# Visits of four feature tiles instead of two for the conditioning products of a two-layer hybrid decoder step

## Chip, cores and metric

The kernel runs on one core of one Trainium2 chip. The metric is the device time of one execution in microseconds; less is better. The core's engines each work through a queue of their own, in order: TensorE (PE in the profile; its weight loads are PEld), VectorE (DVE), ScalarE (ACT), GpSimd (POOL) and SyncE (SP, which here only issues transfers). Times stand as the hardware profiler took them.

## What is computed

One step of a two-layer decoder trunk for 512 prompt tokens and 8 single-token samples, in float32. Each layer takes shift, scale and gate from a conditioning vector, normalises and modulates its input, projects it to the columns of four token mixers, runs these, and adds the gated output projection to the stream:

```python
mod = jax.nn.silu(c) @ ada_w[l] + ada_b[l]
shift, scale, gate = jnp.split(mod, 3, axis=-1)
h = rms_norm(x, norm_g[l]) * (1.0 + scale[:, None, :]) + shift[:, None, :]
proj = h @ w_in[l]
pa, pb, pc, pd = jnp.split(proj, [A_W, A_W + B_W, A_W + B_W + C_W], axis=-1)
...            # oA: HGRN2, oB: RWKV-7, oC: dilated attention, oD: multi-scale pooling
mix = jnp.concatenate([oA, oB, oC, oD], axis=-1).astype(x.dtype)
x = x + gate[:, None, :] * (mix @ w_out[l])
```

Here `c` is (9, 1024) for prompt and samples together, `ada_w[l]` is 1024 x 3072, `w_in[l]` 1024 x 3648 and `w_out[l]` 1024 x 1024. The change concerns the first line: `silu(c) @ ada_w[l]`.

## The kernel before

**Layout.** Features lie on the 128 partitions, tokens along the free side: 520 columns (512 prompt tokens, 8 samples), worked in two halves of 256 and 264. A feature tile is 128 of the 1024 model features, so every product over the model width is a sum over eight feature tiles.

**Projections.** `project` makes one 128-column block of `w_in` or `w_out` at a time. It is carried in three products per feature tile and half (high part of the input by high part of the weights, low by high, high by low), so a block is 48 matmuls ("pj" in the profile). Weights arrive in half blocks of 256 KB in `wraw` and are split into `whi` and `wlo` by ScalarE with GpSimd or with an accumulating transfer; each of these tags has four buffers (`FBUFS`). Loads of weights are issued by SP.

**Conditioning products.** `ada_part(l, f0, nf, spare, ahead, pin)` makes the shift and scale of `nf` feature tiles of layer l, or its gates for `nf == 8`. With 1024 columns it takes the eight feature tiles of `silu(c)` one by one: it loads 512 KB of `ada_w` (tile `adaw`, loaded from SP at L380) and multiplies in four column groups of 32 (`Q4`), which the profile shows as 8 instructions of the form 128*32 128x256 per feature tile, name "ada". The sum goes to SBUF (`adar`), is transposed (`adaT`) and becomes the factors (`mod`). With `ahead` of 1, as in the three parts below, each feature tile's load stands one step ahead of its products. These loads take buffers of the tag `big`, of which there are four; the transposed key caches (`ckT`) use the same tag later.

**The planner.** A layer's mixers are Python generators ("streams"). `Flow` interleaves them with the generator of the projections. A stream that yields `(cost, latency)` tells how much TensorE time, in ns, the step just emitted takes and how long until its next step has its inputs. The cost is added to a clock `t` and, times `RATIO` (1.11), to a debt; while the debt is positive, the planner emits projection steps, 660 each in the usual case, which lower it. Then it emits a step of the ready stream of the lowest priority number. A stream is ready again at `t + latency * LAT` (`LAT` is 1.3).

```python
        cost, lat = r[0:2]
        e[4] = len(r) == 2
        self.t += cost
        e[1] = self.t + lat * LAT
        self.debt = max(self.debt, -2000.0) + cost * self.ratio
```

In layer 0 the streams are B (priority 0), A, CS, C, D, and with the last priority, 5, first `ada_part(0, 0, 8)` (the gates of layer 0), then `ada_next(0)`, which runs `ada_part(1, 0, 4)` and after it `ada_part(1, 4, 4)` (shift and scale of layer 1). The first of these two and the gates can be open at once. Layer 1 has no such stream in its planner. The other conditioning parts are made outside the planner, with `ahead` of 2, 4 or 8, and are told apart by `ahead > 1`.

**The order on the engines.** What the planner emits is a program order. The framework (`schedule_with_timeline_sim=True`) then places each engine's instructions with a timeline of its own, so that an instruction whose inputs are late there is passed by later ones; the result is fixed per engine before the kernel runs. Buffers of a tag are handed out in that order, and a load into one waits, at SP, for its last reader.

Of the kernel before, what the change touches and what calls it, by code (L numbers as in the profile page):

```python
# [191 lines left out]
def trunk(ctx: ExitStack, tc: tile.TileContext, I, O):  # L192
# [28 lines left out]
    def half_t(name):  # L221
        return sb.tile([128, NT], F32, tag="h", name=name, bufs=FBUFS["h"])
# [7 lines left out]
    def sm_ps(name):  # L230
        return ps.tile([128, 512], F32, tag="sm", name=name, bufs=1)
# [10 lines left out]
    def add(out, a, b, eng=V):  # L242
        return tt(out, a, b, ALU.add, eng)
# [9 lines left out]
    def stt(out, a, s, b, op0, op1):  # L253
        return V.scalar_tensor_tensor(out=out, in0=a, scalar=s, in1=b, op0=op0, op1=op1)  # L254
# [5 lines left out]
    def copy(out, a):  # L260
        return A.activation(out, a, AF.Copy)  # L261
# [6 lines left out]
    def mm(out, lhsT, rhs, start=True, stop=True):  # L268
        return PE.matmul(out, lhsT, rhs, start=start, stop=stop)  # L269

    def bc(ap, shape):
        return ap.to_broadcast(shape)
# [40 lines left out]
    def P(l, name, j=0, n=1):  # L313
        a, _ = PCOL[name]
        return par[:, l, a + j:a + j + n]
# [44 lines left out]
    def ada_part(l, f0, nf, spare=0, ahead=1, pin=False):  # L360

        gates = nf == 8

        def pinned(ins):
            return tc.keep_in_program_order(ins) if pin else ins


        c0, width = (2048, 1024) if gates else (256 * f0, 256 * nf)  # L370

        nk = 2 if nf == 1 else 1
        W, kp = width * nk // 4, 1024 // width
        pt = (pj_ps if kp > 1 else sm_ps if l and gates else mm_ps)("ada")[:, 0:W]
        ws = []
        for i in range(8 // kp + ahead):
            if i < 8 // kp:
                w = (f1k if i < spare else big_t)("adaw")
                w = w.rearrange("p (k n) -> p k n", k=kp)
                load(w, I["ada_w"][l, :, i * kp:(i + 1) * kp, c0:c0 + width])  # L380
                ws.append(w)
            if i < ahead:
                if i == ahead - 1:
                    yield 0.0, 0.0
                continue
            for k in range((i - ahead) * kp, (i - ahead + 1) * kp):
                for g in range(4 // nk):
                    r4 = Q4[nk * g + k % nk]
                    mm(pt[r4, :], sc[:, k, :], ws[i - ahead][:, k % kp, W * g:W * g + W],
                       start=(k < nk), stop=(k >= 8 - nk))  # L390
            if ahead > 1:
                yield 450.0, 1500.0
            elif (i - ahead) % 2:
                yield 900.0, 3000.0
        raw = half_t("adar")[:, 0:W]
        pinned(copy(raw, pt))
        yield 0.0, 600.0
        nq = W // 128
        pT = sm_ps("adaT")[:, 0:128 * nq // nk]
        if nk == 1:  # L400
            for q in range(nq):
                PE.transpose(pT[:, q * 128:q * 128 + 128], raw[:, q * 128:(q + 1) * 128], ident)
        else:
            mm(pT, raw, pairs)
        n = 1 if gates else 2
        m = cst.tile([128, n, nf, 9], F32, name=f"mod{l}{f0}{nf}")

        src = pT.rearrange("p (q g f b) -> p f g q b" if nf == 4 else "p (q f g b) -> p f g q b", q=nq, b=32, f=n)
        for f in range(n):
            bias = P(l, "ada_b", 16 if gates else 8 * f + f0, nf).rearrange("p (g q) -> p g q", q=nq)  # L410
            add(m[:, f].rearrange("p (g q) b -> p g q b", q=nq), src[:, f, :, :, 0:9],
                bc(bias[:, :, :, None], [128, nf // nq, nq, 9]))
        if gates:
            modG[l] = m[:, 0]
        else:
            g = P(l, "norm_g", f0, nf)
            stt(m[:, 1], m[:, 1], 1.0, bc(g[:, :, None], [128, nf, 9]), ALU.add, ALU.mult)
            for k in range(nf):
                modS[l, f0 + k], modA[l, f0 + k] = m[:, 0, k, :], m[:, 1, k, :]
        yield 240.0, 600.0  # L420
# [1092 lines left out]
    def layer(l, xs, rstd, x_src, soon, scaled=None):  # L1513
# [49 lines left out]
        def split_projections():  # L1563
# [5 lines left out]
            def make(k):  # L1569
# [8 lines left out]
                if k in (1, 3, 5):  # L1578
                    scaled((k + 1) // 2)

            later = ada_part(l, 4, 4, 8, 8, True)

            def use_part(n, j):
# [17 lines left out]
            for half in range(2):  # L1601
                for gi, group in enumerate([tiles[0:FIRST[0]]] + [[e] for e in tiles[FIRST[0]:]]):
                    g = []
                    for name, _, M, _ in group:
                        n, j = (name, 0) if name == "wa" else (name[:2], int(name[2]))
                        g.append(((l, name), M, use_sum(name, n, j, M) if half else use_part(n, j)))
                    yield from project(g, xt, make if gi == 0 else None, 4 * half, 4 * half + 4)
                    if half:
                        for name, _, _, _ in group:
                            flow.done.add(name)  # L1610
                    else:
                        for _ in range(FIRST[0]):
                            next(later, None)
                if not half:
                    for _ in later:
                        pass
                    small_params()
                    for name in CONST_SHAPES:
                        if name not in C and name not in ("seg", "rope"):
                            load_const(name)  # L1620
                    flow.add(ada_part(l, 0, 8), 5)
# [61 lines left out]
        if not last:  # L1683
            soon = ada_part(l + 1, 0, 8, 4, 8)
            next(soon)
# [163 lines left out]
```

## Time and profile before

| | us |
|---|---|
| median of 3 runs | 762.91 |
| lowest and highest run | 761.4, 771.46 |
| the profiled execution, its own time | 762.74 |
| its span, first to last instruction | 760.9 |

The span is what the profile's rows cover; the execution's own time has 1.8 us more around it. Busy time is per engine, and engines overlap. A row of a timeline gives the start, the duration, the engine, the line and operation, and what is written from what; an "x8" says that eight instructions alike stand in a row, and a bracket how long the engine was idle before the row and what ended that. Matmuls overlap in the pipeline, so the distance between two starts tells what one costs, not its duration. PEclk is the granted share of TensorE's clock.

### The profile page before, as it was taken

To read this page: it belongs to the slowest core of one execution; us is meant where nothing else is said; L and a number is where in the kernel's file an instruction comes from. 1 tells how busy PE (TensorE), PEld (TensorE's weight loads), DVE (VectorE), ACT (ScalarE), POOL (GpSimd) and SP (SyncE) were. 2 spreads that over 40 slices of the span, in tenths; PEclk is the share of its full clock that TensorE was granted. 3 is DMA by queue.
4 is the path that set the end of the run, shared out by engine and by line. 5 is a ranking of instruction groups with operands and counts; after the bars stand their busy time and mean duration, and the time that the engine had idled before them with its cause. 6 is when DMAs were issued, how large, how long until landed. Compare 5 with 4: busy or idle time off the path is not lost. (4 is left out here: it accounts for less than half of the span.)

```text
span 760.9 us, 18617 instructions
## 1 busy us (share of the span) xinstructions
PE 691.9 (91%) x7297; PEld 615.1 (81%) x7297; DVE 505.1 (66%) x1183; ACT 457.6 (60%) x988; POOL 281.8 (37%) x326
## 2 busy tenths in 40 slices
PE   2899998997989899998998989898698999998997
PEld 1687777897889888877797889797697989787897
DVE  4547627989985454787456352995999763577863
ACT  5255787535645566895355899943264557688641
POOL 1344213427732223136326232454454232213641
PEclk9999999998999979999999999999798999999999
DMA  9968887887664539579794678799755448459575
GB/s 325 350 228 291 289 234 166 212 210 180 145 168 96 145 104 261 152 181 295 161 258 129 148 159 177 169 207 223 181 122 143 102 106 215 97 143 277 118 172 152
DMA packets 87608, 142.46 MB, mean 187 GB/s; under 512 B 20577, under 2 KB 29089, under 8 KB 87521
## 3 DMA queue, kind: packets, MB, share of 16 engines
q1 hardware_dynamic: 67216, 104.50, 42.6%
q0 software_dynamic: 20160, 36.71, 28.3%
q8 instruction: 57, 0.93, 0.5%
q14 instruction: 31, 0.25, 0.1%
q10 hardware_dynamic: 144, 0.06, 0.0%
HBM read 88.20 MB, written 14.22 MB: 135 GB/s over the span
## 5 line engine op out<-in xcount | busy, mean ns | idle before, releaser
L269 PE MATMUL pj<-hh,whi 128*128 128x256 f32 (+1 forms) x928 | 270.6, 299 | 10.9 <-ACT hh L261 4.9
L269 PE MATMUL pj<-hh,wlo 128*128 128x264 f32 (+1 forms) x896 | 259.6, 294 | 10.3 <-DMA wlo<-wraw 10.1
L269 PE MATMUL pj<-hl,whi 128*128 128x256 f32 (+1 forms) x928 | 264.7, 291 | 2.7 <-issue 1.3
L462 POOL DMA_DIRECT2D wlo<-wraw x128 | 115.7, 928 | 269.7 <-ACT wlo L461 180.5
L269 PEld LDWEIGHTS pj<-hh,whi 128*128 128x128 f32 x928 | 178.0, 194 | 24.9 <-issue 7.7
L269 PEld LDWEIGHTS pj<-hh,wlo 128*128 128x128 f32 x896 | 172.2, 194 | 17.1 <-DMA wlo<-wraw 12.2
L269 PEld LDWEIGHTS pj<-hl,whi 128*128 128x128 f32 x928 | 178.5, 194 | 6.0 <-issue 2.9
L261 ACT ACTIVATE whi<-wraw 128x512 fp32r<-128x512 f32 (+1 forms) x146 | 91.2, 627 | 122.5 <-PE pj L269 111.6
L461 ACT ACTIVATE wlo<-whi 128x512 fp32r<-128x512 f32 x128 | 80.4, 634 | 1.8
L269 PE MATMUL pj<-ml,whi 128*128 128x256 f32 (+1 forms) x256 | 72.5, 285 | 2.7 <-DVE cst L250 2.7
L269 PE MATMUL pj<-mh,whi 128*128 128x256 f32 (+1 forms) x256 | 73.1, 291 | 0.2 <-ACT mh L261 0.2
L269 PE MATMUL pj<-mh,wlo 128*128 128x256 f32 (+1 forms) x256 | 71.9, 283 | 0.0
L254 DVE SCALAR_TENSOR_TENSOR x<-pj,mod,x 128x256 f32<-128x256 f32 x64 | 30.9, 483 | 41.3 <-PE pj L269 40.9
L269 PEld LDWEIGHTS pj<-ml,whi 128*128 128x128 f32 x256 | 48.2, 188 | 4.4 <-DVE ml L237 3.4
L269 PEld LDWEIGHTS pj<-mh,whi 128*128 128x128 f32 x256 | 47.6, 188 | 4.1 <-issue 2.8
L269 PEld LDWEIGHTS pj<-mh,wlo 128*128 128x128 f32 x256 | 48.1, 188 | 0.8 <-issue 0.8
L269 PE MATMUL ada<-adaw,sc 128*32 128x256 f32 (+1 forms) x448 | 34.4, 379 | 15.4 <-DMA adaw<-in_ada_w_dram 15.4
L237 POOL TENSOR_TENSOR wlo<-wraw,whi 128x512 fp32r<-128x512 f32 x16 | 23.9, 1500 | 38.3 <-ACT whi L261 35.3
L237 POOL TENSOR_TENSOR gate<-gate,raw 128x520 f32<-128x520 f32 x16 | 21.6, 1348 | 42.1 <-issue 18.8
L269 PEld LDWEIGHTS ada<-adaw,sc 128*32 128x32 f32 x448 | 12.8, 115 | 24.2 <-DVE nacc L237 12.4
L269 PE MATMUL alv<-aqz,ak 128*64 128x64 f32 x384 | 20.2, 247 | 8.2 <-DVE ak L237 7.9
L269 PEld LDWEIGHTS alv<-aqz,ak 128*64 128x64 f32 x384 | 16.8, 156 | 11.3 <-issue 6.9
(394 smaller groups left out, 1388.8 us busy)
## 6 DMA issues: line engine op xcount, KB each, us to landing
wlo<-wraw POOLq DMA_DIRECT2D x128, 256.0 KB, 4.2
wraw<-in_w_in_dram SPq DMA_DIRECT2D x112, 256.0 KB, 3.6
adaw<-in_ada_w_dram SPq DMA_DIRECT2D x48, 512.0 KB, 6.2
wraw<-in_w_out_dram SPq DMA_DIRECT2D x32, 256.0 KB, 3.4
x<-in_x_dram SPq DMA_DIRECT2D x8, 520.0 KB, 6.4
ckT<-in_ckT_dram SPq DMA_DIRECT2D x8, 320.0 KB, 4.6
x<-xmid SPq DMA_DIRECT2D x4, 520.0 KB, 6.8
cvr<-in_cvr_dram SPq DMA_DIRECT2D x4, 512.0 KB, 6.4
```

What stands on the lines that cost most here:

```text
L237: return eng.tensor_tensor(out=out, in0=a, in1=b, op=op)
L254: return V.scalar_tensor_tensor(out=out, in0=a, scalar=s, in1=b, op0=op0, op1=op1)
L261: return A.activation(out, a, AF.Copy)
L269: return PE.matmul(out, lhsT, rhs, start=start, stop=stop)
L461: A.activation(lo, hi.bitcast(F32), AF.Copy, scale=-1.0)
L462: G.dma_start(out=lo, in_=w, accum_op=ALU.add)
```

## The change

In the loop of `ada_part`, the branch for `ahead` of 1 yielded to the planner behind every second feature tile, with a cost of 900 and a latency of 3,000. Now it yields behind every fourth, with 1,800 and 6,000. A visit thus emits four feature tiles: their 32 product instructions and, of the loads, the three that belong to its second to fourth tile and the one of the next visit's first. A part of eight tiles has two visits instead of four. Nothing else is edited.

```diff
             if ahead > 1:
                 yield 450.0, 1500.0
-            elif (i - ahead) % 2:
-                yield 900.0, 3000.0
+            elif (i - ahead) % 4 == 3:
+                yield 1800.0, 6000.0
         raw = half_t("adar")[:, 0:W]
         pinned(copy(raw, pt))
         yield 0.0, 600.0
```

## Rows read from the trace of the kernel before

**Rows 1.** The page, part 1: busy time, share of the span, instructions.

```profile
PE 691.9 (91%) x7297; PEld 615.1 (81%) x7297; DVE 505.1 (66%) x1183; ACT 457.6 (60%) x988; POOL 281.8 (37%) x326
```

**Rows 2.** Instructions on tile adaw, 55 to 113 us: duration ns min/median/max; landing us.

```profile
L269 PE MATMUL ada<-adaw,sc x192: 379/379/634, 55.6 to 112.3; 128*32 128x256 f32 x192
...
DMA to landing us min/median/max: 3.7/4.7/6.2
```

**Rows 3.** Stretches of the span; the first row names the columns.

```profile
core 0: us, PE busy (x) PEld busy (x) DVE busy (x) ACT busy (x) POOL busy (x), PEclk, DMA share, GB/s
55.00:113.00 58.00, 55.91 (x491) 43.03 (x492) 34.58 (x76) 40.10 (x79) 16.64 (x12) 0.97 0.85 269
113.00:405.00 292.00, 274.54 (x3028) 244.44 (x3026) 206.59 (x489) 171.63 (x375) 111.98 (x123) 0.96 0.73 183
```

**Rows 4.** Timeline of TensorE around two runs of ada products.

```profile
70.36 0.28 PE L269 MATMUL pj<-hh,wlo 128*128 128x264 f32 x1
70.57 0.64 PE L269 MATMUL ada<-adaw,sc 128*32 128x256 f32 x8
71.14 0.39 PE L269 MATMUL pj<-hh,whi 128*128 128x264 f32 x1
...
98.07 1.07 PE L269 MATMUL ada<-adaw,sc 128*32 128x256 f32 x16
99.07 0.39 PE L269 MATMUL pj<-hh,whi 128*128 128x256 f32 x1
99.30 0.28 PE L269 MATMUL pj<-hl,whi 128*128 128x256 f32 x1
99.42 0.28 PE L269 MATMUL pj<-hh,wlo 128*128 128x256 f32 x1
```

**Rows 5.** The same timeline: first and last of 20 runs, and a piece.

```profile
55.62 1.50 PE L269 MATMUL ada<-adaw,sc 128*32 128x256 f32 x24
...
62.19 0.62 PE L269 MATMUL ada<-adaw,sc 128*32 128x256 f32 x4
...
112.01 0.64 PE L269 MATMUL ada<-adaw,sc 128*32 128x256 f32 x8
```

**Rows 6.** SP's own waits, 36 to 128 us: us in total, times, longest.

```profile
SPq L380 <- PE ada L269: 20.8, 14, 3.8
```

**Rows 7.** Timeline of TensorE, 103 to 107 us.

```profile
103.20 1.03 PE L269 MATMUL ada<-adaw,sc 128*32 128x256 f32 x8 [1.79 <-DMA adaw<-in_ada_w_dram]
104.16 0.59 PE L269 MATMUL pj<-hh,whi 128*128 128x264 f32 x1
104.55 0.42 PE L269 MATMUL pj<-hl,whi 128*128 128x264 f32 x1
...
106.53 0.38 PE L269 MATMUL pj<-hl,whi 128*128 128x264 f32 x1
```

**Rows 8.** A stretch behind that wait, columns as in rows 3.

```profile
104.20:106.50 2.30, 2.30 (x13) 2.30 (x11) 0.00 (x0) 0.32 (x1) 0.68 (x1) 0.50 1.07 276
```

**Rows 9.** TensorE's waits, 113 to 405 us: us in total, times, longest.

```profile
PE pj L269 <- DMA wlo<-wraw: 4.2, 5, 1.9
```

**Rows 10.** Timelines of four engines, 110 to 128 us.

```profile
122.86 0.39 PE L269 MATMUL pj<-hh,whi 128*128 128x264 f32 x1 [3.68 <-ACT raw L261]
...
123.84 0.42 PE L269 MATMUL pj<-hl,whi 128*128 128x264 f32 x1
...
127.14 0.32 PE L269 MATMUL pj<-hl,whi 128*128 128x264 f32 x1
...
121.19 1.07 ACT L258 ACTIVATE brn<-bsq 128x1040 f32<-128x1040 f32 x1 [2.96 <-DVE bsq L250]
...
110.72 0.49 DVE L250 TENSOR_SCALAR ak<-ak,omlb 128x520 f32<-128x520 f32 x1
...
117.61 2.96 DVE L250 TENSOR_SCALAR ak<-ak,omlb 128x520 f32<-128x520 f32 x1
...
117.78 2.49 POOL L687 MEMSET aqz<- 128x1024 f32 x2
```

## The prediction

> **What bounds the kernel now.** I read the page's first part, then a table of stretches of the span. TensorE is busy for 691.9 of 760.9 us, and of the engines that compute beside it none reaches 70% [rows 1]. So a change pays when it takes work off TensorE's queue or time out of its waits. The conditioning products ("ada") come in several stretches, and I looked for those that the edited branch makes. Between 55 and 113 us there are 192 of them [rows 2], which is three parts of eight feature tiles with 8 instructions each (four column groups, two instructions per group): the gates of layer 0 and the two `ada_part(1, ...)` calls of `ada_next(0)`. All others are made with `ahead` of 2, 4 or 8 and don't reach the edited line. In this stretch TensorE is busy for 55.9 of 58 us and the DMA engines for 0.85 [rows 3]. Nothing is hidden under an idle TensorE here: each 0.1 us saved is 0.1 us of the span, as long as nothing else takes it.
>
> Next, the timeline of TensorE in that stretch. Most runs of ada products that stand among the projections have 8 or 16 instructions, one tile or two. One of 8 lasts 0.57 us to the next projection (70.57 to 71.14), one of 16 lasts 1.00 (98.07 to 99.07). So a tile costs 0.43 us, and 0.57 - 0.43 = 0.14 us is a charge per run. Around a run more is lost: from the last projection to ada takes 0.21 us (70.36 to 70.57) and from the first projection behind it to the second 0.23 (99.07 to 99.30), where two projections in a row are 0.12 apart (99.30 to 99.42). That is 0.09 and 0.11 [rows 4]. **One switch to ada and back costs 0.14 + 0.09 + 0.11 = 0.34 us, beside 0.43 us per tile.**
>
> The stretch holds 20 such runs, from 55.62 to 112.01 [rows 5]. Twelve visits of two tiles would be 12 runs. They are 20, because the scheduler puts each tile where it expects its weights to have landed, not where the visit stands in the program: nine runs of 8, three of 16, two of 24 (one of them with a wait inside), and six pieces of a tile, which cut three tiles in two. A piece of 4 lasts 0.62 us where a whole tile lasts 0.64 [rows 4, 5], so each cut also costs a second 0.43. The 20 switches cost 6.8 us, the 24 tiles 10.3, the three cuts 1.3.
>
> Then the loads. One lands 4.7 us (median) after its issue [rows 2], and around this stretch SP waits 20.8 us, in 14 pieces of at most 3.8, for ada products to release one of the four `big` buffers [rows 6]. TensorE itself waited for a load once, 1.79 us at 103.20 [rows 7].
>
> **The change, part by part.**
>
> *Fewer visits.* Per part two visits instead of four, 6 instead of 12 in all. The declared cost per part stays (4 x 900 = 2 x 1,800), and so does the declared delay (4 x 3,000 = 2 x 6,000), so the planner should end each part about where it did. No instruction is added or removed: the same 192 products, 24 loads, 3 copies of the sums.
>
> *Fewer switches.* From below: all visits whole, 6 runs, 14 x 0.34 = 4.8 us saved, and 1.3 more if no tile is cut. From above: each tile by itself, 24 runs, 4 x 0.34 = 1.4 us lost. Which end is nearer follows from the buffers. There are four; a visit finds its first tile loaded and issues four more loads, three of its own and the next visit's first. While both the gates and the first `ada_next` part are open, the other part holds one buffer. So at most three tiles are there at the visit's start; the fourth load needs the first tile's release and lands 4.7 us later [rows 2]. A visit therefore breaks at least once, 12 runs in all, and up to 18 if it breaks twice. I take 15, with the cuts as they are: **5 x 0.34 = 1.7 us saved.**
>
> *Loads.* Their order within a part is unchanged, but three of a visit are due at once where one was. The wait at 103.20 cost 1.79 us, and behind it TensorE ran at the lower of its two clocks (1.2 GHz, a granted share of 0.50): the eight ada products took 0.96 us instead of 0.57, the first projection 0.39 to the next instead of 0.23, and from 104.55 to 106.53 nine more were 0.22 apart instead of 0.12 [rows 7, 8]. That is 0.39 + 0.16 + 0.9 = 1.5 us, and 3.3 with the wait. From below -3.3; from above +3.3 for each further one, at most one for each of six visits. I take none more and none less, since 23 of 24 tiles are placed behind enough projections today. **0.**
>
> *SP's queue.* A visit's loads stand in SP's order ahead of weights loads (`wraw`), and two of them, the fourth and the fifth, wait for products of the same visit. A weights load behind them comes up to one such wait later, 3.8 us at most so far [rows 6]. In this stretch no projection waited for its weights, so their lead covers what already happens. Cost 0, and if the lead is used up one set of weights waits like those further on, 4.2 us in 5 pieces [rows 9].
>
> *Streams in between.* While a visit of 1,800 ns runs, the other streams' next products come up to 0.9 us later, and after it the projections get 1,800 x 1.11 = 2.0 us in a row, double of before. The dense TensorE of the stretch covers the copies and scans that this delays. The last of these products runs at 112 us [rows 5], and the layer-1 factors that it feeds are first used behind 405 us, so that end has slack. What may move is the order of everything that is planned after the first visit. The trace shows what one accident of order costs: at 122.86 TensorE idles for 3.68 us because ScalarE waited 2.96 us for VectorE, which took 2.96 us for an operation that takes 0.49 elsewhere, while GpSimd cleared a buffer. From 123.84 to 127.14 fifteen projections then take 3.3 us where fifteen at 0.12 take 1.8: 1.5 more, 5.2 in all [rows 10]. I take 0, with such a stall either way as bound.
> The Trainium skill ("SBUF — State Buffer", section "SBUF: two separate sides") says that VectorE in some modes and GpSimd share a pair of ports as an exclusive lock, so that the loser waits for the other's whole instruction. The trace agrees as far as it goes: 2.96 is 0.49 on top of a GpSimd span of 2.49. By the rule such a meeting costs a whole instruction or nothing, by the order alone.
>
> *Sum.* The profiled execution took 762.74 us, of which 760.9 are span; the median of the runs is 762.91, 0.2 more. 762.74 - 1.7 + 0 + 0 + 0 = **761.0 us**. A measurement of this kernel can tell about 2% from no change, 15.3 us.
>
> **Rivals.**
>
> *The scheduler cuts the visits as before* (the change hardly does what it says). For it: only three of twelve visits are plain runs of 16 today, and the buffers set the pace. Against it: the first run, three tiles at 55.62, shows that loaded tiles do stay together [rows 5]. 20 runs, 762.7 us.
>
> *Whole visits and no wait.* Against: it needs four landed tiles in four buffers. 762.7 - 4.8 - 1.3 - 3.3 = 753.3 us.
>
> *Bursts wait for their loads* (slower). A visit whose fourth, or third and fourth, tile is placed too early stops TensorE, whose queue is in order. Place: the second half of each visit, above all in the last part, where the one wait already is. Price 3.3 us each. For it: DMA is busy for 0.85 of the stretch [rows 3]. Against: 1 of 24 so far. Six visits with a wait are five more than now: 762.7 + 16.5 = 779.2 us. Five further waits are needed to pass 2% (16.5 against 15.3); three make 772.6.
> The Trainium skill ("TensorE: Matmul & The Clock Gate", section "HAM oscillation — how this bites in real kernels") describes a kernel whose short burst per tile is followed by a wait for the next load, and which falls back to the low clock at every tile. Here the one wait shows the same fall [rows 7]; by that rule every visit that waits would pay it, which is this rival's 779.2.
>
> *The rest of layer 0 is replanned.* One stall like that of 122.86 less is 755.8, one more 766.2, two more 771.4. From 113 to 405 us TensorE is idle for 292 - 274.5 = 17.5 us [rows 3], so such things can be won and lost.
>
> **How the numbers follow.** Forecast (12 to 18 runs, 757 to 765 us): 0.42. Visits cut as before, 763: 0.18. Whole visits, 753: 0.08. Replanned to the better: 0.08, of which 0.04 by three stalls or more (745). To the worse: 0.12, of which 0.02 by four stalls or more (782). Waits for loads: 0.12, of which 0.08 with five or more further ones. So faster 0.04, slower 0.02 + 0.08 = 0.10, same 0.86. The range goes from 753 (whole visits) to 773 (three further waits, or two stalls more); it leaves out 0.04 below and about 0.10 above.
>
> **What would show it.** Right: 12 to 18 runs of ada products between 55 and 113 us, runs of 24 or 32 instructions among them, at most two waits of TensorE for `adaw` there, the stretch 1 to 2 us shorter. Wrong: 20 runs or more (no switch saved); four or more waits for `adaw` with projections 0.22 apart behind them; or the same time up to 113 us and more idle time of TensorE between 113 and 405. The stretch from 405 us on should keep its length within about 2 us, since no visit lies in it.

## The result, and the profile after

The changed kernel takes 770.5 us (median; 768.59 to 777.47) beside 766.0 us (761.4 to 771.46) for the kernel before in the same comparison. The medians lie 4.5 us (0.6%) apart; the ratio formed over the runs, by which this text goes, is 1.0105, 95% interval [1.0085, 1.0125]: about 1% slower, which is 8 us. The time lies inside the range that was given, but not where it was forecast, and on the other side of the old one. The two profiled executions, 762.74 and 771.28 us, lie 8.5 us apart: the one before is among the shorter of its kernel's runs.

Part 1 of the page of the changed kernel, whose execution took 771.28 us with a span of 769.5:

```profile
PE 699.1 (91%) x7297; PEld 618.9 (80%) x7297; DVE 503.5 (65%) x1183; ACT 457.0 (59%) x988; POOL 282.5 (37%) x326
```

The instructions are the same in number [rows 1]. TensorE is busy 7.2 us longer with them. The stretches of the span show where; the first row names the columns, and the cuts behind 113 us are each kernel's own first projection of layer 1 (421 after, 408 before). First the changed kernel, then the kernel before.

```profile
core 0: us, PE busy (x) PEld busy (x) DVE busy (x) ACT busy (x) POOL busy (x), PEclk, DMA share, GB/s
55.00:113.00 58.00, 56.90 (x495) 42.87 (x496) 40.37 (x87) 41.84 (x80) 15.05 (x12) 1.00 0.87 279
113.00:421.00 308.00, 280.68 (x3027) 247.12 (x3025) 204.72 (x484) 172.43 (x380) 113.15 (x125) 0.94 0.70 173
421.00:770.00 349.00, 323.04 (x3413) 298.30 (x3413) 232.86 (x541) 219.80 (x478) 136.97 (x163) 0.96 0.67 161
```

```profile
113.00:408.00 295.00, 275.70 (x3032) 245.04 (x3030) 207.85 (x492) 174.37 (x382) 112.94 (x126) 0.97 0.73 183
408.00:761.00 353.00, 323.10 (x3413) 297.60 (x3411) 236.72 (x540) 219.90 (x477) 134.90 (x162) 0.97 0.65 158
```

Three things are to be seen. The stretch with the visits is better than before: TensorE busy for 56.90 us where it was 55.91, granted clock 1.00 for 0.97 [rows 3]. The loss lies behind it, where no product was moved: from 113 us to layer 1 it takes 308 us for 295. Of these 13, 8.0 are idle time of TensorE (27.3 for 19.3) and 5.0 are longer busy time for the same work (3,027 and 3,032 recorded matmuls, in another order), at a granted clock of 0.94 for 0.97. And layer 1 gives back 4 of them.

The products themselves, on tile adaw between 55 and 113 us (duration ns min/median/max, first and last start), changed kernel:

```profile
L269 PE MATMUL ada<-adaw,sc x192: 379/379/403, 56.0 to 105.8; 128*32 128x256 f32 x192
```

They are done 6.5 us earlier than in [rows 2], and the wait for a load is 0.41 us instead of 1.79 [rows 7]. But they come in 23 runs instead of 20, and five tiles are cut in two instead of three.

TensorE's waits between 113 us and layer 1 (total us, times, longest), first the changed kernel, then the kernel before (its 4.2 us for `wlo` stand in [rows 9]):

```profile
PE alv L269 <- DVE ak L237: 5.1, 3, 4.1
PE pj L269 <- DMA wlo<-wraw: 5.1, 4, 2.4
PE cT L1259 <- DVE cS L250: 4.8, 2, 4.0
PE bXT L269 <- issue: 2.5, 1, 2.5
PE cT L1259 <- DVE dS L237: 1.5, 1, 1.5
```

```profile
PE pj L269 <- ACT raw L261: 3.7, 1, 3.7
PE bs L269 <- DVE bslo L237: 2.3, 1, 2.3
PE alv L269 <- DVE ak L237: 0.7, 1, 0.7
```

The stall at 122.86 us [rows 10] is gone. In its place TensorE waits 15.9 us for VectorE in this stretch (all such groups together), where it waited 6.7.

**What VectorE does then.** Its timeline (start us, us, operation, idle time before it and what ended that) at 149 us in the changed kernel, then the same instructions in the kernel before:

```profile
152.33 0.76 DVE L237 TENSOR_TENSOR bMB<-bA,c_mb 128x256 f32<-128x256 f32 x2 [1.18 <-PE bA L269]
162.12 0.76 DVE L237 TENSOR_TENSOR sAk<-sv,ak 128x256 f32<-128x256 f32 x2 [9.04 <-DMA sv<-sv0A]
162.80 0.75 DVE L237 TENSOR_TENSOR bMB<-bA,c_mb 128x256 f32<-128x256 f32 x2
163.46 4.33 DVE L1004 STREAM_TRANSPOSE bsq<-bMB 32x512 f32<-32x512 f32 x4
```

```profile
157.04 2.50 DVE L237 TENSOR_TENSOR bMB<-bA,c_mb 128x256 f32<-128x256 f32 x6 [0.38 <-PE bA L269]
159.46 4.32 DVE L1004 STREAM_TRANSPOSE bsq<-bMB 32x512 f32<-32x512 f32 x4
165.37 0.76 DVE L237 TENSOR_TENSOR sAk<-sv,ak 128x256 f32<-128x256 f32 x2 [1.59 <-DMA sv<-sv0A]
```

Stream A's step on the sample states (`sAk`, line 722) needs values that make a round trip through DRAM (`svt`, `sv0A`, `sv`). In the kernel before it stands behind stream B's `bMB` products and transposes. In the changed kernel it has slipped ahead of the last of them, and VectorE, which works in order, idles for 9.04 us with stream B's work behind the waiting instruction. The planner explains the slip: with a visit declared as 1,800 in one piece, stream B's steps from the 16th on come two projection steps later. When its 26th step (the first `bA`) is still not due, stream A's 8th is, and it is taken 14 projection steps earlier than before. The sums of declared costs end at the same place in both kernels. In layer 1 the planner's list is the same, step for step; what the engines run there is not: TensorE's order differs from the 50th instruction of the layer on, since the framework places all of it anew.

A second place lies near 350 us. Timelines of VectorE and of GpSimd in the changed kernel:

```profile
346.94 4.34 DVE L251 TENSOR_SCALAR by<-by,par 128x520 f32<-128x520 f32 x2
351.20 1.19 DVE L250 TENSOR_SCALAR cS<-cS,cst 128x384 f32<-128x384 f32 x1
...
346.13 1.93 POOL L237 TENSOR_TENSOR cres<-cres,again 128x520 f32<-128x520 f32 x1 [2.56 <-ACT cres L261]
348.63 2.35 POOL L237 TENSOR_TENSOR dt<-du 128x527 f32<-128x527 f32 x2
```

In the kernel before the two `by<-by,par` take 1.01 us together (at 334.42). Here they take 1.41 and 3.01, and each ends about 0.3 us behind GpSimd work (348.35 behind `cres`, 348.06; 351.3 behind the second of two `dt`, 350.98). The `cS` behind them comes late, and TensorE waits the 4.0 us for it that the table of waits shows. The Trainium skill ("SBUF — State Buffer", section "SBUF: two separate sides") says that VectorE in some modes and GpSimd share a pair of ports as a lock that is held for a whole instruction. The first duration agrees; the second began ahead of both `dt` (348.3) and lasted past both, which is more than one instruction, as far as these spans of GpSimd are exact.

What this place is worth shows in a stretch around it, first the changed kernel, then the kernel before:

```profile
340.00:370.00 30.00, 23.62 (x178) 19.81 (x177) 22.93 (x48) 16.09 (x34) 14.07 (x13) 0.83 0.62 186
```

```profile
340.00:370.00 30.00, 27.89 (x235) 24.01 (x234) 21.71 (x56) 15.17 (x30) 15.78 (x16) 1.00 0.94 256
```

TensorE idles 6.4 us in it for 2.1, and its granted clock is 0.83 for 1.00. All waits ahead of `cT` products in layer 0 come to 7.8 us in the changed kernel and to none in the kernel before.

### The profile page after: what moved, and what is told of

It reads as the page before. It is cut to its first block, busy times and chain, and to the rows that moved or that the text cites. A ratio compares the mean times of both kernels' runs of the same rounds, so it can differ in the third digit from the quotient of the medians.

```text
span 769.5 us, 18608 instructions
## 1 busy us (share of the span) xinstructions
PE 699.1 (91%) x7297; PEld 618.9 (80%) x7297; DVE 503.5 (65%) x1183; ACT 457.0 (59%) x988; POOL 282.5 (37%) x326
## 5 line engine op out<-in xcount | busy, mean ns | idle before, releaser
L269 PE MATMUL pj<-hh,wlo 128*128 128x264 f32 (+1 forms) x896 | 258.9, 293 | 10.4 <-DMA wlo<-wraw 10.1
L462 POOL DMA_DIRECT2D wlo<-wraw x128 | 116.2, 916 | 259.1 <-ACT wlo L461 168.5
L269 PEld LDWEIGHTS pj<-hh,whi 128*128 128x128 f32 x928 | 177.5, 195 | 20.9 <-issue 10.4
L269 PEld LDWEIGHTS pj<-hh,wlo 128*128 128x128 f32 x896 | 172.1, 194 | 15.9 <-DMA wlo<-wraw 12.7
L269 PE MATMUL pj<-mh,whi 128*128 128x264 f32 (+1 forms) x256 | 73.4, 293 | 1.0 <-ACT mh L261 1.0
L269 PE MATMUL pj<-mh,wlo 128*128 128x264 f32 (+1 forms) x256 | 71.6, 283 | 0.0
L269 PE MATMUL ada<-adaw,sc 128*32 128x256 f32 (+1 forms) x448 | 36.9, 391 | 12.8 <-DVE nacc L237 12.4
L269 PE MATMUL alv<-aqz,ak 128*64 128x64 f32 x384 | 20.2, 249 | 11.2 <-DVE ak L237 10.8
```

Source lines behind the costliest of these rows:

```text
L462: G.dma_start(out=lo, in_=w, accum_op=ALU.add)
```

## The experiments

Theories at the start. **W**: the loss is the order of the steps behind the visits, above all the one wait of 9.04 us. **Rivals**: the visits themselves (later loads, later products), or where single tiles fall. All ratios are to the kernel before on the same chip, with 95% intervals. Edits are to the kernel named.

**1. Visits of four, old order** (kernel before). With 900 and 3,000 declared twice per visit, the planner's list is that of the kernel before, but the first yield of a visit carries all four tiles.

```
-            elif (i - ahead) % 2:
+            elif (i - ahead) % 4 == 3:
+                yield 900.0, 3000.0
                 yield 900.0, 3000.0
```

> Visits of four feature tiles, but the planner is told of four steps of 900 and 3,000 per part as before (the two steps of a visit follow each other without products between), so the planner's whole list of steps is the one of the kernel before; only the place of the ada products and their loads in it is changed. Theory R (the loss comes from the changed order of the streams behind the visits): no loss, 764 to 768 us (ratio 0.997 to 1.003), stretch from 113 us to the end of layer 0 as long as before, about 292 us. Theory V (the loss comes from the visits themselves, through their loads, buffers and SP's queue): the loss stays, 769 to 772 us (ratio 1.005 or more).

Measured: 0.9914 [0.9879, 0.9948], 758.6 us. Visits of four by themselves need not cost; with the old list they are faster than either kernel. The stretches:

```profile
55.00:113.00 58.00, 57.46 (x514) 45.02 (x507) 35.52 (x78) 41.99 (x82) 17.45 (x13) 1.00 0.87 275
113.00:400.00 287.00, 268.93 (x3002) 240.63 (x3001) 204.98 (x488) 169.85 (x375) 112.27 (x123) 0.97 0.74 185
400.00:753.00 353.00, 324.18 (x3413) 298.57 (x3413) 236.76 (x541) 220.32 (x478) 134.88 (x163) 0.97 0.66 159
```

There are 20 runs of ada products, so no switch was saved. Gone are the wait for `adaw` and the stall at 122.86; in the stretch to layer 1 TensorE waits 6.2 us for `wlo` (4.2 before) and 2.6 us at `cT` (none before) instead.

**2. Visits of four, 7,000 declared** (changed kernel, 7,000 for 6,000). The streams' steps come in the order of the kernel before; only stream B's first steps move, by one or two projection steps.

> Visits of four as in the changed kernel, with a declared delay of 7,000 instead of 6,000. With this number the planner's order of the streams behind the visits comes out as in the kernel before, to within a step or two of the projections. Theory R: 763 to 768 us (ratio 0.997 to 1.003). Theory V: 769 to 772 us, as the changed kernel, since visits, loads and buffers are the same.

Measured: 1.0069 [1.0040, 1.0098]. Against W, in its narrow form and in its wide one: `sAk` stands where it stood before, the visits are of four as in experiment 1, the list is the old one to within two projection steps, and a loss is there nonetheless. TensorE waits once for 4.9 us (`bss<-bbon`, at 123 us) and once for 4.3 us (`wlo`).

**3. Visits of two, new order** (changed kernel). The planner's list is exactly the changed one, but the last two tiles of a visit enter the program two projection steps behind it.

```
+                if (i - ahead) % 4 > 1: deferred.append(products)
```

> The planner's list of steps is exactly that of the changed kernel, but a visit emits two feature tiles at once and the other two only after two projection steps. Theory R: the loss stays without visits of four, 769 to 772 us (ratio 1.005 to 1.013), and the stretch from 113 us to the end of layer 0 is about 9 us longer than before. Theory V: 764 to 768 us (ratio 0.997 to 1.003).

Measured: 1.0074 [1.0039, 1.0108]. The new list carries a loss of this size without visits of four, with both places in it: VectorE waits 9.6 us at `sAk`, and TensorE waits 4.0 us at `cT`.

**4. Visits of two, 3,600 declared** (kernel before, 3,600 for 3,000), which gives nearly the changed order.

> The kernel before with visits of two and one number changed: a declared delay of 3,600 instead of 3,000. With it the planner's order behind the visits comes out as in the changed kernel, to within a step of the projections. Theory R: 769 to 772 us (ratio 1.005 to 1.013). Theory V: 764 to 768 us (ratio 0.997 to 1.003).

Measured: 1.0237 [1.0198, 1.0275]. A declared number alone, with no product and no load changed, costs 2.4%. The size of the loss does not follow from the list alone, since the changed kernel, with nearly this list, loses 1.0%.

**5. The early step held back** (changed kernel, layer 0).

```
         yield from to_tokens(vtm, v)
+        if l == 0:
+            yield "a_hold"
...
-        y_s = sample_read(S0s, zq)
+        y_s = sample_read(S0s, zq); flow.done.add("a_hold")
```

> The kernel after, with one step of layer 0 held back: stream A's first step on the sample states (its two VectorE products sAk wait for values that come back through DRAM) may not be put into the program before stream B's eight steps of products bA are in it, which is where the kernel before has it. The planner's list is then that of the kernel before, with streams A and B two projection steps later from stream B's 16th step on. Theory W (the loss is the 9.04 us that VectorE stands at the head of its queue for sv while stream B's work lies behind it): the VectorE wait of sAk for sv falls from 9.0 to under 3.5 us, the stretch from half to 70% of the in-projection's products comes back from 74.9 to 66 to 69 us, and the median stands at 0.992 to 1.003 of the kernel before. Theory S (the loss is in the small shifts of one to three steps and in where four tiles fall, as the kernel with 7000 made it likely at 1.007): 1.006 or more, whatever sAk waits.

Measured: 1.0105 [1.0044, 1.0165]. The wait fell as it should, and the time didn't. The waits at `cT` are 1.0 us here, so in this list neither of the two places is left, and others cost as much. VectorE's and TensorE's waits (125 to 170 us, and 113 us to layer 1):

```profile
DVE sAk L237 <- DMA sv<-sv0A: 3.0, 2, 2.0
```

```profile
PE pj L269 <- DMA wlo<-wraw: 9.2, 5, 3.0
PE alv L269 <- DVE ak L237: 4.9, 3, 3.2
```

**6. The early step alone** (kernel before): stream A's 8th step gets the planner's precedence, 14 projection steps earlier; all other steps stay within ten.

```
-        yield from to_tokens(vtm, v)
+        yield from ((*y, 1) if l == 0 and y[1] else y for y in to_tokens(vtm, v))
```

> The kernel before (visits of two, its own declared numbers), with one step of layer 0 brought forward: stream A's first step on the sample states gets the planner's precedence and stands ahead of stream B's eight steps of products bA, as in the kernel after; 14 projection steps earlier, and all else within three or four steps. Theory W: the wait of sAk for sv on VectorE goes from 1.6 to 7 us or more, half to 70% of the in-projection takes 70 us or more where it took 64.8, and the ratio to the kernel before is 1.006 to 1.014 with not one visit changed. Theory S: the visits are untouched, so 0.997 to 1.003.

Measured: 1.0203 [1.0147, 1.0259], more than either theory gave. TensorE now waits behind VectorE at the very place:

```profile
PE bA L269 <- DVE bMB L237: 4.0, 1, 4.0
```

```profile
DVE sAk L237 <- DMA sv<-sv0A: 7.5, 1, 7.5
```

**7. The wait moved to GpSimd** (changed kernel, order unchanged).

```
-                mul(sflat(kv)[:, :, t], vb[:, :, t], scols(k[:, :, SM], i)[:, :, t])
+                mul(..., eng=G if l == i == 0 else V)
```

> The kernel after with its order of steps exactly, but the two products sAk of stream A's first step on the sample states in layer 0 are done by GpSimd in place of VectorE, so that GpSimd and not VectorE stands and waits for sv. Theory W: no VectorE wait for sv ahead of bA's products, half to 70% of the in-projection back from 74.9 to 64 to 69 us, ratio 0.994 to 1.003; the two products take some us longer on GpSimd, which is off the path there. Theory S: the order of steps is that of the kernel after, so 1.007 to 1.013. If the tail (the waits of about 4 us for the tiles cT near 350 us) stays while half to 70% comes back, the tail has a cause of its own in the order of steps, and the ratio lies between, at 1.001 to 1.006.

Measured: 1.0091 [1.0053, 1.0130]. TensorE's order up to layer 1 is that of the changed kernel, instruction for instruction. VectorE's wait for `sv` falls to 3.5 us, but VectorE waits 5.2 us for stream B's `bA` products in that order, and the tail stays: TensorE waits 4.0 us at `cT`. The second pair of `sAk`, still on VectorE, takes 4.29 us for 0.76 beside GpSimd's, and stream B's `bZ` behind it starts at 165.7 us where it was 168.5: the edit frees 2.8 of the 9 us.

**8. The early step with visits of four** (experiment 1 with the edit of experiment 6).

> Visits of four with the order of steps of the kernel before (0.991 of the kernel before), and with stream A's first step on the sample states brought forward as in the kernel with that one edit. Theory W: the price of the early step is the same with visits of four as with visits of two, so 0.997 to 1.005, against 0.991 without it. Theory S: 0.989 to 0.994.

Measured: 1.0110 [1.0056, 1.0165], against 0.9914 without it. The step costs the same 2% with either size of visit. TensorE's longest wait is 7.0 us, for `bslo`.

**9. Late fours, old order** (kernel before). The first of two yields brings no products, the second brings four tiles.

```
+            j = i - ahead
+            late = range(j // 4 * 4 * kp, (j + 1) * kp) if j % 4 == 3 or j == 8 // kp - 1 else ()
-            for k in range((i - ahead) * kp, (i - ahead + 1) * kp):
+            for k in late if ahead == 1 else range((i - ahead) * kp, (i - ahead + 1) * kp):
```

> The kernel before with its order of steps and its yields exactly, but the first yield of a visit of four tiles comes without products and the second brings the products of all four (in the kernel with visits of four and the old order, 0.991, the first brought all four). Visits of four by themselves, then, and two tiles of each visit one half visit later than in the kernel before. Theory V (what sets the end is VectorE's work and waits between 113 us and the first product for bXT, and the visits matter only as far as they disturb that): VectorE's idle time there stays that of the kernel before or of the kernel with the early four, 7 to 11 us, bXT starts at 206 to 214 us, ratio 0.988 to 1.003. Rival T (it is the time at which the tiles are taken, on TensorE, that decides): the products come later, the parts end later and the wait at 122.86 us (3.68 us) grows: 1.003 or more.

Measured: 0.9964 [0.9925, 1.0002]. Here the runs really do join, 11 instead of 20, and TensorE pays for it in waits for loads (its waits from 55 to 113 us):

```profile
PE ada L269 <- DMA adaw<-in_ada_w_dram: 5.4, 5, 2.2
```

Nine switches less are 9 x 0.34 = 3.1 us; 5.4 - 1.8 = 3.6 us of waits are more. The waits also come with a lower granted clock, 0.91 where it was 0.97 in the kernel before, and TensorE is busy for 50.29 of these 57 us where it was 55.21:

```profile
56.00:113.00 57.00, 50.29 (x431) 39.94 (x428) 38.65 (x80) 42.11 (x78) 15.63 (x12) 0.91 0.71 227
```

So the exchange that the prediction weighed is real, and in the visits' own stretch it loses. What the kernel shares with experiment 1 is the old list. In the same profile VectorE idles for 8.5 us at `aqz`, TensorE's first `bXT` starts at 223 us instead of 212, and layer 1 begins 4.3 us later (411.95 for 407.70). The time isn't longer because layer 1 itself is 8.7 us shorter, which nothing in the edit explains. Whether VectorE's waits ahead of `bXT` set the end of layer 0 therefore stays open.

**10 and 11. VectorE's time, priced** (kernel before). The same amount of repeated work with the same result at two places of layer 0: the transposes `bsq<-bMB` three times (8.6 us more, spread from 161 to 185 us), or the subtraction `ckl` seven times (8.3 us more, from 279 us).

```
-        for i, r4 in enumerate(Q4):
+        for i, r4 in list(enumerate(Q4)) * (3 if l == 0 else 1):
```

```
-                sub(kl[th][r, pp], x, ks[th][r, pp].bitcast(F32), eng=V)
+                for _ in range(7 if l == th == 0 else 1):
+                    sub(kl[th][r, pp], x, ks[th][r, pp].bitcast(F32), eng=V)
```

> The kernel before, where in layer 0 the four stream transposes bsq<-bMB on VectorE (4.32 us at 159.46 us) are done three times over, with the same result: 8.64 us more of VectorE's time at the place where the changed kernel has it waiting 9.04 us for sv; nothing of the planner or of the visits is touched. Theory V: VectorE has no slack until bXT, so bXT starts 6 to 9 us later than at 212.0 (what is taken off is its two waits of 1.6 and 1.1 us for sv right behind) and the ratio is 1.007 to 1.013. Rival T (VectorE's waits are a sign of a late TensorE and DMA, not the cause): TensorE was busy in all of 140 to 165 us, so most of it hides: 0.999 to 1.004.

> The kernel before, where in layer 0 two subtractions ckl<-ck,cks on VectorE (0.69 us each, at 278.96 and 280.77 us) are done seven times over, with the same result: 8.3 us more of VectorE's time behind bXT, where VectorE is busy for 7.13 of 20 us. Theory V: the work there lies in VectorE's idle time, ratio 0.998 to 1.003. Rival: any 8 us on VectorE cost as much wherever they lie, 1.007 or more.

Measured: 1.0136 [1.0093, 1.0178] and 1.0037 [0.9995, 1.0080]. Early on, 8.6 us of VectorE cost 10.4 us; later 8.3 us cost 2.8, with no cost at all inside the interval. In the first, TensorE stands and waits:

```profile
PE bZ L269 <- DVE bX L237: 9.5, 1, 9.5
```

The two are not prices of VectorE's time alone. The planner's list is untouched, but the framework answers the longer work with another order: TensorE's leaves that of the kernel before at 179 us in experiment 10 and at 287 us in 11. The early addition was dear, and added time and new order are not told apart.

**12. The tail's meeting taken away** (changed kernel): `by<-by,par` of layer 0 on ScalarE.

```
+            if l == 0:
+                act(y[:, j, :], y[:, j, :], AF.Identity, scale=P(l, "gn_w", j), bias=P(l, "gn_b", j))
+                continue
             ts(y[:, j, :], y[:, j, :], P(l, "gn_w", j), ALU.mult, P(l, "gn_b", j), ALU.add)
```

> The kernel after, where in layer 0 the two VectorE instructions by<-by,par (line 1165; 1.41 and 3.01 us at 346.9 us, beside two GpSimd instructions of 1.93 and 2.35 us that end when they end; 0.54 us each in the kernel before) are done by ScalarE; the planner's list is untouched. Theory P (the tail of the loss is this meeting of VectorE with GpSimd: TensorE then waits 4.04, 0.80 and 1.54 us for cS and dS in the kernel after and not at all in the kernel before): the wait of 4.0 us for cS is gone, TensorE waits under 2 us for VectorE at cT, and the ratio to the kernel before goes from 1.0105 to 1.003 to 1.007. Rival Q (the streams are late by then anyway and the wait is only a sign of it): another wait of 3 us or more stands in its place and the ratio stays at 1.008 to 1.013.

Measured: 1.0107 [1.0073, 1.0141]. Timelines of VectorE, GpSimd and TensorE:

```profile
345.95 2.89 DVE L250 TENSOR_SCALAR cS<-cS,cst 128x512 f32<-128x512 f32 x1
348.76 5.93 DVE L237 TENSOR_TENSOR by<-by,again 128x520 f32<-128x520 f32 x4
...
346.20 2.35 POOL L237 TENSOR_TENSOR dt<-du 128x527 f32<-128x527 f32 x2
...
356.19 1.08 PE L1262 MATMUL cT<-c_ident,cS 128*128 128x128 f32 x4 [6.57 <-DVE dS L237]
```

The meeting has moved to the next instruction: now `cS` takes 2.89 us beside GpSimd, and TensorE waits 6.57 us where it waited 4.04 and 1.54. All waits at `cT` come to 9.8 us for 7.8: the tail was not taken away, so this run does not say what the tail costs.

**13. Both at once** (changed kernel with the edits of 7 and 12).

> The kernel after with both named waits taken off at once: by<-by,par of layer 0 on ScalarE, and the two products sAk of stream A's first step on the sample states on GpSimd (that alone: 1.0091, with VectorE's wait for sv down from 9.0 to 3.5 us). Theory P: the two are the loss, and the ratio comes back to 0.997 to 1.004. Rival Q: the loss is spread over many small waits that this order of steps brings, 1.006 or more whatever single wait is taken away.

Measured: 1.0116 [1.0057, 1.0176]. The time is what rival Q gave, but the tail is still there; TensorE's waits and its stretch from 340 to 370 us:

```profile
PE cT L1262 <- DVE dS L237: 6.6, 1, 6.6
```

```profile
340.00:370.00 30.00, 21.68 (x182) 17.59 (x180) 24.20 (x49) 16.18 (x37) 15.36 (x13) 0.83 0.64 189
```

The waits at `cT` are 9.8 us, as in experiment 12. What 7, 12 and 13 show is that easing VectorE's wait for `sv` gains nothing that is clear of the noise, and that the edit of 12 does not remove the tail. All kernels with the new list (after, 3, 4, 7, 12, 13) have 7.5 to 10.4 us of waits at `cT`, all others at most 2.9. That the tail is the loss of these kernels is a rival that no run here tests.

**All side by side.** TensorE's waits from 113 us to layer 1 are summed over the trace of each profiled execution, short ones included.

| kernel | ratio | TensorE's waits, us | of these for VectorE |
|---|---|---|---|
| 1 fours, old order | 0.991 | 16.8 | 8.2 |
| 9 late fours, old order | 0.996 | 20.1 | 11.2 |
| before | 1 | 17.8 | 6.7 |
| 11 VectorE later | 1.004 | 23.5 | 9.3 |
| 2 fours, 7,000 | 1.007 | 25.6 | 13.3 |
| 3 twos, new order | 1.007 | 28.5 | 18.1 |
| 7 GpSimd waits | 1.009 | 24.5 | 15.1 |
| **after** | 1.0105 | 26.0 | 15.9 |
| 5 held | 1.0105 | 25.5 | 9.5 |
| 12, 13 | 1.011, 1.012 | 28.2, 29.1 | 16.7, 16.5 |
| 8 fours, early step | 1.011 | 30.4 | 22.2 |
| 10 VectorE at 160 us | 1.014 | 26.7 | 18.1 |
| 6 early step | 1.020 | 28.8 | 19.9 |
| 4 twos, 3,600 | 1.024 | 32.1 | 23.4 |

The kernels that aren't slower have at most 20.1 us, those that are shown slower at least 24.5; experiment 11, whose interval includes no change, has 23.5. A single profile is only good to some us here: experiment 11 runs the program of the kernel before up to 279 us, and its wait for `adaw` at 102.93 is 3.46 us where that was 1.79 [rows 7], and its first `bXT` starts at 217.1 us where that was 212.0; over the same TensorE instructions from 113 to 279 us its waits come to 18.2 us where they were 13.9. So the gap between the two groups is no wider than the spread of one program.

## Why the prediction was wrong, step by step

**What bounds the kernel.** Right for the stretch of the visits, and it ended too soon. The condition "as long as nothing else takes it" is where the time went.

**Fewer switches, -1.7 us.** Wrong. 5 fewer runs were forecast; the changed kernel has 3 more, which is +1.0 us by the same 0.34, and two more cut tiles, 0.9 us by the same 0.43; experiment 1 has the same 20. The reason given for the 20, that a tile is placed where its weights are expected, also decides against the whole visits. Only the late fours joined them, and paid in waits what they saved.

**Loads, 0 between -3.3 and +3.3.** The value was too cautious, the bound was good: the wait fell from 1.79 to 0.41 us and the half clock behind it is gone (granted 1.00). The rival of bursts that wait did not come; it appears in experiment 9, at 5.4 us.

**SP's queue, 0.** Right: projections waited 5.1 us in 4 pieces for `wlo`, where it was 4.2 in 5 [rows 9].

**Streams in between, 0 with a stall of 5.2 us either way.** This is the step that failed. It argued that a dense TensorE covers the streams' delay up to 112 us, put the order behind that at 0, and bounded it by one stall either way. The equal sums of declared cost do not keep the order: the last part ends 4 projection steps earlier than before, stream B's steps come two steps later, and one step of stream A 14 steps earlier. With this list the kernel is 1.0% slower, with visits of two 0.7% (experiment 3), and with the old list and the same visits 0.9% faster (experiment 1). In the profile the stretch from 113 us to layer 1 became 13 us longer, with 4 us back in layer 1. Why layer 1 is shorter was not tested; the forecast that it keeps its length within 2 us was wrong as well.

**The price of an accident** was right in size. Experiment 1 no longer has the two that the prediction had priced, 3.3 and 5.2 us, together 8.5, and its profiled execution is 754.62 for 762.74, 8.1 less. That the two agree so well is in part luck: this execution is the shortest of its 11, the medians lie 6.4 us apart, and other waits came and went. The changed kernel lost the same two and got others; it is 1.9% above experiment 1 (1.0105/0.9914). That the 0.9% belongs to visits of four is not shown: no switch was saved, and experiment 2, with the same visits and almost the same list, is 0.7% slower than the kernel before. Beside the stall at 122.86 the prediction set a rule of one whole instruction; its GpSimd span of 2.49 us is two `aqz` clears, which begin 0.17 us behind the VectorE instruction [rows 10].

**The rivals.** "Replanned, to the worse" is what happened; two more stalls would be 771.4, and 770.5 was measured. That the two are so near is luck: the prediction's base of 762.7 rests on three runs, and twenty give 766.0, from which 770.5 is less than one stall away, and 8 us by the ratio less than two. Its chance of 0.12 was too small: nothing in the profile spoke for the same order of so many steps being kept, and all five other lists that were run (the changed kernel's, 2, 4, 5 and 6) are slower, whatever the size of the visits. The signs named for it, 20 runs or more and more idle time of TensorE behind 113 us, are those that came.

**What stays open.** Why the old order is the better one has no single answer in these runs. One early step suffices for 2% (6, 8), but it is not needed (2, 5). Easing VectorE's wait for `sv` in the changed kernel's list gained nothing that is clear of the noise (7), but took only a part of it away. The tail near 350 us comes with the new list in all six of its kernels, and no run took it away there; other lists lose as much without it (5, 6, 8). So it is shown that a changed list alone costs 0.7 to 2.4% (3, 4, 6) and that more than one set of waits can make up such a loss; which property of the order makes them is not. Nor is it shown how much of it is the planner's list and how much the framework's placement: TensorE's order up to layer 1 changed with every edit but that of 7, also where the list stayed as it was (10, 11, 12).

## What to carry to other kernels

When a planner places the work, a change of a declared cost is a change of order everywhere behind it, and that must be priced first: here the same visits measured 0.9% faster with the old list and 1.0% slower with the new one. Keep the declared steps and move only the work that hangs on them (experiment 1) to see the one without the other. Look in the changed order for an instruction that waits on a DRAM round trip and now stands ahead of ready work on an in-order engine, but don't expect that removing the longest wait gives it back: look first whether the waits of the bounding engine shrink in sum. And before an experiment is read as the removal of a wait, check in its own trace that the wait is gone.

## What the runs showed of the hardware

Moving `by<-by,par` from VectorE to ScalarE did not end the meeting with GpSimd, it passed it on: `cS<-cS,cst` then took 2.89 us and four `by<-by,again` 5.93, beside GpSimd's `dt` and `dS`. Whether moving the string of GpSimd instructions instead would help was not tested.

TensorE's waits can cost more than their length. From 113 us to layer 1 the same products took 280.68 us of busy time at a granted clock of 0.94, and 275.70 at 0.97: 5.0 us beside 8.0 us of further waits. The Trainium skill ("TensorE: Matmul & The Clock Gate", section "HAM oscillation — how this bites in real kernels") describes a kernel whose waits between bursts let TensorE fall to the low clock; the granted clock here agrees in direction. The size is no rule: in experiment 13 TensorE idles 11.3 us more than before in this stretch (30.6 for 19.3) and is busy for the same time (275.4 us each, up to the first projection of layer 1), at a clock of about 0.95.
